# Moving the gate rows and gate columns ahead, and the query split behind a unit, in a hybrid attention and mLSTM layer

## The chip, the cores and the metric

The kernel runs on one core of one Trainium2 chip. The metric is the device time of one execution in microseconds; lower is better. The arithmetic is float32 throughout: matrix products are made as three products of a high part and a low part of each operand (marked float32r), so that every weight and every activation is split before it is used.

## The reference, cut to what matters

One layer of a trunk: a SwiGLU half step, token mixing, a second half step. Token mixing makes one projection of the normalised tokens (640 = 512 latent + 128 context) and runs two mixers on it, a differential attention with 8 heads and a bidirectional mLSTM with 4 heads:

```python
mq, mk, mv, mo, mg, dq, dk, dv, gm, gd = split_cols(h @ p['w_in'][l])
dq = rmsnorm(dq...); dk = rmsnorm(dk...)           # then rope for latent tokens
s = einsum('bqhcd,bkhcd->bhcqk', q, k) * scale      # c = 0, 1
pr = softmax(s); w = pr[:, :, 0] - lam * pr[:, :, 1]
att = einsum('bhqk,bkhv->bqhv', w, v)
gates = (mg + b_gate)                               # 16 columns: log_i, log_f
log_f = log_sigmoid(gates[:, 1])                    # then the mLSTM, chunk by chunk:
b = cumsum(fc); a = b + m
m_t = maximum(a, max(b[t] - b[s] + ic[s]))
```

The change touches the attention heads and the gates of the mLSTM (cumulative sums, running maxima and their exponentials), which the mLSTM needs only after the last attention head.

## The kernel before, in words

The stages follow one another: opening and first half step, input projections by a Strassen-like scheme (class Gates), attention (650 to about 1090 us), mLSTM, branch and output projections, second half step. The change lies in the attention stage.

**Units.** While the heads run, PE is kept full with the remaining input projections, cut into units of 24 matmuls or so: `fill.units(n)` (class Fill, line 1245 on) runs the next n of them. The first 20 are narrow token units (values, keys, queries, values: five each; 128x256, one of four PSUM slots of the pool `psum`). Then come wide units in pairs of halves: the two halves of one token block gather in one 128x512 tile, tag "wide", of which there is one (`wide_ps`); behind the second half ACT copies it out in two pieces. Then units by feature. `fill.ahead` loads and splits weights for later units; a split is a copy on ACT (wH) and a subtraction on DVE (wL). `Fill.one` first does the subtractions that wait (`prefetch(0)`).

**A head** (class Head, line 1650) works in five query blocks. `turn_keys` and `turn_queries` transpose a head's tokens on PE, copy them out on ACT into a tile of tag "asq" (one buffer) and spread them by four DMAs into the tile qk_d. `queries` splits qk_d into qT (one ACT copy, one DVE subtraction), `keys` splits the cached and new keys into kH and kL. `scores(qi)` makes eight matmuls into the one score tile "sc" (three PSUM banks, one buffer) and a minimum on DVE; `soft` the exponentials on ACT; `mix` the combination on DVE; `turn(qi)` the transposes of the mixed weights and their copy on ACT (wT); `values(qi)` the products with the values (ps_o) and their scaling on DVE. `finish` transposes the head's output into aT, again of tag "asq", and stores it.

In block qi the order on PE is scores(qi), turn(qi - 1), n[0] units, values(qi - 1), in blocks 2 and 3 the next head's turn_keys and turn_queries, n[1] units. Behind block 4 stands the boundary to the next head N: N.queries, turn(4), N.keys(0), one unit, values(4), N.keys(1, 2), and two more units (lines 2129 to 2144).

**The gates.** gate_products puts the 16 gate columns into PSUM (ps_g, in the score tile's place). `gate_rows` (line 1426), a generator in six parts, makes of them rows of 640 tokens: sums and logarithms, scans, and at its end stores to DRAM (nm_dram, dc_dram, four stores to qq_dram). `gate_load(j)` (1505) reads half j of qq_dram into QQ, a tile of tag "asq"; `gate_cols` (1508) transposes it on PE (ps_c, five transposes) and copies the columns out on DVE.

**Order.** PE's instructions run as written. What ACT, DVE and SP do is put in order by the framework's planner from its own estimate of durations, except inside `with written():`, where each engine's instructions follow one another as written (`placed`, line 37), and except `tc.issue_after(x)`, which puts instructions behind x on x's engine. So before the loop over the heads the unpinned instructions of units, keys, queries and gate rows are mixed by the planner; the gate rows' first part is held behind the split of head 0's keys and queries (line 2064). Their further parts are called in head 0 by `aside` (ROWS, line 2069), which is called twice in each block, before the n[0] units (part 0) and behind values (part 1). gate_load(0) is called in head 2, block 1, gate_cols in head 2, block 2; the second half in head 4. The pool of the gate rows is closed in head 0, block 2 (`begin_pools`).

Of the kernel before, what the change touches and what calls it, by code (L numbers as in the profile page):

```python
# [8 lines left out]
F32R = mybir.dt.float32r  # L9
# [22 lines left out]
def tile_trunk(ctx: ExitStack, tc: tile.TileContext, a: dict):  # L32
# [17 lines left out]
    def act(*args, **kw):  # L50
        return placed(nc.scalar.activation(*args, **kw))  # L51

    def tt(eng, out, in0, in1, op):
        return placed(eng.tensor_tensor(out=out, in0=in0, in1=in1, op=op))  # L54
# [13 lines left out]
    @contextmanager  # L68
    def written():
        was, as_written[0] = as_written[0], in_row  # L70
        yield
        as_written[0] = was
# [4 lines left out]
    def tr(*args, **kw):  # L77
        tc.keep_in_program_order(nc.tensor.transpose(*args, **kw))  # L78
# [23 lines left out]
    def load(pool, shape, src, **kw):  # L102
        t = pool.tile(shape, F32, **kw)
        dma(t, src)
        return t
# [360 lines left out]
    class HalfStep(Winograd):  # L466
# [102 lines left out]
        def run_first(self, x, gate, final, between, ahead, freed):  # L569
# [107 lines left out]
            for j in range(1, 4):  # L677
                for f in range(2):
                    unit(2, j, f, 1)
                    final(2 * j + f, 1)  # L680

        def run(self, x, gate, final, ahead, aside, add_pair):


# [724 lines left out]
    fill = Fill()  # L1409


    def gate_products():
        raw = load(rawp, [128, KT, 128], a["w_g"], tag="raw", name="wg_raw")
        wgH = wide_p.tile([128, KT, 128], F32R, tag="BH", name="wgH", bufs=2)
        wgL = wide_p.tile([128, KT, 128], F32R, tag="BL", name="wgL", bufs=2)
        act(wgH, raw, AF.Copy)
        tt(vec, wgL, raw, wgH.bitcast(F32), ALU.subtract)
        ps = ps_s.tile([128, 1536], F32, tag="sc", name="ps_g")

        def step(hf, k):  # L1420
            cs = half(hf)
            mm3(ps[:, 512 * hf : 512 * hf + HALF], wgH[:, k, :], wgL[:, k, :], hH[:, k, cs], hL[:, k, cs], k == 0, k == KT - 1)

        return ps, step
# [80 lines left out]
    def gate_load(j):  # L1505
        Q_at[0] = j, load(ap, [128, T], qq_dram[:, j, :], tag="asq", name="QQ")

    def gate_cols():
        j, Q = Q_at[0]
        for i0, n in ((0, 4), (4, 1)):  # L1510
            p = psum.tile([128, 4, 128], F32, tag="mm", name="ps_c")
            for i in range(n):
                tr(p[:, i, :], Q[:, (i0 + i) * 128 : (i0 + i + 1) * 128], ident)
            vec.tensor_copy(
                cols[:, i0 : i0 + n, 2 * j : 2 * j + 2, :].rearrange("p i q (d h) -> p i (q d) h", d=2),
                p[:, :n].rearrange("p i (b c) -> p i b c", c=32)[:, :, :, 0:4],
            )
# [63 lines left out]
    def rotate():  # L1581

        if not rotations:
            return False
        first, second = rotations[0], rotations[1] if len(rotations) > 1 else []
        had, left = len(first), len(second)
        with written():
            if had == 4 and left == 7 or had == 2 and left == 5:
                second.pop(0)()
            else:  # L1590
                first.pop(0)()
                if (had, left) in ((5, 8), (4, 6)):
                    second.pop(0)()
            if not first:
                rotations.pop(0)
        return True
# [53 lines left out]
    class Head:  # L1650
# [28 lines left out]

        def queries(self):  # L1680
            self.qT = ap.tile([128, 2, T], F32R, tag="qT", name="qT")
            self.kH = ap.tile([128, 2, 896], F32R, tag="kH", name="kH")
            self.kL = ap.tile([128, 2, 896], F32R, tag="kL", name="kL")
            self.ao = ap.tile([128, 5, 128], F32, tag="ao", name="ao")
            self.at_q = act(self.qT, self.qd, AF.Copy)
            r = slice(64, 128)
            tt(vec, self.qT[r], self.qd[r], self.qT[r].bitcast(F32), ALU.subtract)

        def keys(self, *parts):
            for n in parts:  # L1690
                c0, c1 = ((512, 768), (0, 512), (768, 896))[n]
                v = (self.ck, self.kd[:, :, 0:NS], self.kd[:, :, NS:T])[n]
                act(self.kH[:, :, c0:c1], v, AF.Copy)
                self.at_vec = tt(vec, self.kL[:, :, c0:c1], v, self.kH[:, :, c0:c1].bitcast(F32), ALU.subtract)
# [92 lines left out]
    def begin_pools():  # L1787
        gates.close()
        late_p.append(late_of.enter_context(tc.tile_pool(name="late", bufs=1, reuse_waits="tile")))
        fill.spare = late_p[0]  # L1790
# [3 lines left out]
    def begin_memory():  # L1794
        assert not rotations and not any(isinstance(g[0], tuple) for g in fill.q)
        fill.spare = None
        late_of.close()
        in_pools["k"] = ctx.enter_context(tc.tile_pool(name="mlk", bufs=1, side="right", reuse_waits="tile"))
        load_keys(0)
        load_queries(0)  # L1800
# [168 lines left out]
    with tc.issue_after(box["normed"]):  # L1969
        ps_g, gate_step = gate_products()  # L1970

    heads = [Head(hd) for hd in range(8)]
# [80 lines left out]
    ap = att.enter_context(tc.tile_pool(name="att", bufs=1, reuse_waits="tile"))  # L2053
    rope_p[0] = ap
    gt = gates.enter_context(tc.tile_pool(name="gates", bufs=1))
    heads[0].load_cache()
    heads[0].turn_keys()
    fill.units(1)
    heads[0].turn_queries()
    fill.units(2)  # L2060
    heads[0].queries()
    heads[0].keys(0, 1, 2)
    fill.units(4)
    with tc.issue_after(heads[0].at_vec.ins), tc.issue_after(heads[0].at_q.ins):
        rows = gate_rows(gt, ps_g)
        next(rows)
    fill.units(2)
    fill.eager = False
    ROWS = {(0, 0): 1, (1, 0): 1, (1, 1): 1, (2, 0): 2}

    def aside(hd, qi, part):
        if hd == 0:
            for _ in range(ROWS.get((qi, part), 0)):
                next(rows, None)
        if part == 0:
            with written():
                split = fill.low()
            if qi < 4 and (UNITS[hd][qi][1] or not split):
                rotate()
        elif qi != 3:  # L2080
            rotate()
        if (qi, part) == (1, 1) and hd in (2, 4):
            gate_load(hd // 2 - 1)
        if (qi, part) == (2, 0) and hd in (2, 4):
            gate_cols()

    two, one = (1, 1), (1, 0)
    UNITS = {hd: (two, one, two, one, one, (1, 1, 1)) for hd in range(7)}
# [3 lines left out]
    for hd in range(8):  # L2092
        H = heads[hd]
        odd = hd % 2
        N = heads[hd + 1] if hd < 7 else None
        for qi in range(5):
            n = UNITS[hd][qi]
            with written():
                H.scores(qi)
                if qi > 0:  # L2100
                    H.turn(qi - 1)
                H.soft(qi)
            aside(hd, qi, 0)
            fill.units(n[0])
            with written():
                H.mix(qi)
            if late is not None and qi == 1:
                with written():
                    late()
                late = None  # L2110
            if qi > 0:
                with written():
                    H.values(qi - 1)
            if qi in (2, 3) and hd < 7:
                with written():
                    (N.turn_keys, N.turn_queries)[qi - 2]()
            if qi == 3 and hd < 7:
                N.load_cache()
            aside(hd, qi, 1)
            if (hd, qi) == (0, 2):  # L2120
                begin_pools()
            elif (hd, qi) == (6, 2):
                begin_memory()
            fill.units(n[1])
            if n[1]:
                rotate()
            with written():
                fill.ahead()
        n = UNITS[hd][-1]
        if hd < 7:  # L2130
            with written():
                N.queries()
                H.turn(4)
                N.keys(0)
            fill.units(n[0])
            with written():
                H.values(4)
                N.keys(1, 2)
            H.finish_norm()
            fill.units(n[1])  # L2140
            with written():
                fill.ahead()
            fill.units(n[2])
            late = H.finish
        else:
            with written():
                H.turn(4)
            fill.eager = True
            fill.units(1)
            H.values(4)  # L2150
            H.finish_norm()
            fill.drain(3)
            with written():
                H.finish()
# [543 lines left out]
```

## Time and profile before

| | us |
|---|---|
| median of three runs | 1822.37 (1822.31 to 1822.61) |
| profiled execution | 1822.42 |
| its span | 1820.6 |
| attention stage, about 650 to 1090: PE busy | 411.4 of 440 |

A row of a timeline has its start in us from the start of the span, the time it took, the engine, the line, the operation, the tile written <- the tiles read, sizes, the number of instructions merged and, in brackets, how long the engine stood idle before it and whose result ended that. In a list of waits the columns are: who waited for whom, the total, how often, the longest. In a table of windows each engine has its busy time and, in parentheses, its instructions; then come the mean granted clock of TensorE (1.00 is full), the share of the DMA engines and the GB/s. PE is TensorE, DVE VectorE, ACT ScalarE, SP the engine that issues most DMAs.

### The profile page before, as it was taken

How to read it: one execution, taken by the hardware profiler on the slowest of the kernel's cores; microseconds unless marked ns; L12 is line 12 of the kernel's file. 1: busy time of each engine (PE TensorE's matmuls, PEld its weight loads, DVE VectorE, ACT ScalarE, POOL GpSimd, SP SyncE). 2: the span in 40 equal slices, each digit the busy share in tenths (PEclk: the TensorE clock that was granted, in tenths of full speed). 3: DMA queues.
4: the chain of work that ended last, by engine and by line, in shares of the span. 5: the costliest groups of instructions: out<-in, count | busy, mean ns of one | idle time of the engine just before them, and what ended most of it. 6: DMA issues, size and time to landing. Idle time of an engine off the chain costs nothing.

```text
span 1820.6 us, 29424 instructions
## 1 busy us (share of the span) xinstructions
PE 1772.2 (97%) x11790; PEld 1706.0 (94%) x11790; DVE 1341.5 (74%) x2136; ACT 894.2 (49%) x1563; POOL 40.8 (2%) x72
## 2 busy tenths in 40 slices
PE   8999999999999998989899999999999999999998
PEld 6999999999999998868788998899999999999998
DVE  6889986677889748667675546876767888997485
ACT  5654553342655445555554536563326545454432
POOL 0000000100000000000000000000000000000010
PEclk9999999999999999999999999999999999999999
DMA  8255566977236554233334336566652445557992
GB/s 331 105 197 185 184 222 237 346 225 258 76 138 202 179 173 105 85 90 107 90 112 129 109 105 234 178 228 212 233 171 80 134 164 193 195 183 272 354 311 82
DMA packets 150075, 328.32 MB, mean 180 GB/s; under 512 B 11633, under 2 KB 107633, under 8 KB 138161
## 3 DMA queue, kind: packets, MB, share of 16 engines
q1 hardware_dynamic: 138562, 280.69, 45.8%
q0 software_dynamic: 10688, 43.13, 7.4%
q10 hardware_dynamic: 688, 2.63, 0.4%
q8 instruction: 92, 1.51, 0.3%
q14 instruction: 45, 0.37, 0.1%
HBM read 243.77 MB, written 72.15 MB: 174 GB/s over the span
## 4 chain that ended last, share of the span: by engine, by line
PE 80%; DMA 7%; DVE 7%; ACT 4%; issue 1%; SPq 1%; ACTq 0%; DVEq 0%
PE ps_f L75 49%; PE ps_p L75 14%; PE ps_t L75 7%; PE sc L75 2%; PE ps_o L75 2%; DVE ww L54 2%; DMA qk_d<-qk_t 1%; PE ps_n L75 1%; DMA P<-nm_dram 1%; DMA raw_a<-in_w_ada_k 1%; DMA raw<-in_w2b 1%; PE ps_wT L78 1%; DVE junk L814 1%; PE ps_u L75 1%; SPq L1668 1%
## 5 line engine op out<-in xcount | busy, mean ns | idle before, releaser
L75 PE MATMUL ps_f<-S,ww 128*128 128x320 f32 x2400 | 387.1, 309 | 2.8 <-DMA S<-g_dram 0.9
L75 PEld LDWEIGHTS ps_f<-S,ww 128*128 128x128 f32 x2400 | 359.8, 188 | 6.9 <-DVE ww L54 4.6
L54 DVE TENSOR_TENSOR ww<-raw,ww 128x2048 fp32r<-128x2048 f32 (+1 forms) x73 | 163.9, 2245 | 66.0 <-ACT ww L51 65.9
L75 PE MATMUL ps_f<-hm,ww 128*128 128x320 f32 x1176 | 185.7, 309 | 0.1
L75 PEld LDWEIGHTS ps_f<-hm,ww 128*128 128x128 f32 x1176 | 175.7, 188 | 0.5 <-DVE ww L54 0.5
L51 ACT ACTIVATE ww<-raw 128x2048 fp32r<-128x2048 f32 (+1 forms) x73 | 136.8, 1875 | 59.2 <-DVE raw L54 34.9
L54 DVE TENSOR_TENSOR raw<-raw 128x1024 f32<-128x1024 f32 x186 | 160.6, 863 | 2.4
L75 PE MATMUL ps_f<-hm,wB 128*128 128x320 f32 x1008 | 161.5, 309 | 0.0
L75 PE MATMUL ps_t<-wH,hH 128*128 128x256 f32 (+1 forms) x440 | 152.8, 347 | 7.4 <-ACT stage L51 2.9
L75 PE MATMUL ps_p<-hH,wH 128*128 128x320 f32 x480 | 150.7, 314 | 1.5 <-DVE num L54 1.5
L75 PEld LDWEIGHTS ps_f<-hm,wB 128*128 128x128 f32 x1008 | 151.3, 188 | 0.0
L75 PE MATMUL ps_t<-wH,hL 128*128 128x256 f32 (+1 forms) x440 | 147.7, 336 | 0.9 <-DVE hL L54 0.9
L75 PE MATMUL ps_p<-hH,wL 128*128 128x320 f32 x480 | 148.3, 309 | 0.0
L75 PE MATMUL ps_p<-hL,wH 128*128 128x320 f32 x480 | 148.3, 309 | 0.0
L75 PE MATMUL ps_t<-wL,hH 128*128 128x256 f32 (+1 forms) x440 | 147.8, 336 | 0.0
L51 ACT ACTIVATE u<-ps_f 128x320 f32<-128x320 f32 x129 | 55.7, 432 | 155.5 <-PE ps_f L75 155.3
L54 DVE TENSOR_TENSOR wL<-raw,wH 128x2048 fp32r<-128x2048 f32 x37 | 84.6, 2287 | 35.5 <-ACT wH L51 34.4
L75 PEld LDWEIGHTS ps_t<-wH,hH 128*128 128x128 f32 x440 | 85.2, 194 | 16.2 <-ACT stage L51 3.5
L51 ACT ACTIVATE wH<-raw 128x2048 fp32r<-128x2048 f32 (+1 forms) x45 | 75.4, 1682 | 50.4 <-PE ps_p L75 36.1
L54 DVE TENSOR_TENSOR wB<-raw,wB 128x1024 fp32r<-128x1024 f32 x64 | 78.0, 1218 | 26.1 <-ACT wB L51 26.1
L814 DVE CUSTOM_DVE_ANT_0 junk<-raw_a,csil 128x1024 bf16<-128x1024 f32 (+1 forms) x76 | 92.5, 1217 | 3.6 <-DMA raw_a<-in_w_ada_c 3.3
L75 PEld LDWEIGHTS ps_t<-wH,hL 128*128 128x128 f32 x440 | 84.8, 193 | 10.1 <-DVE hL L54 1.1
(304 smaller groups left out, 3536.0 us busy)
## 6 DMA issues: line engine op xcount, KB each, us to landing
g_dram<-g SPq DMA_DIRECT2D x44, 640.0 KB, 7.7
raw_a<-in_w_ada_c POOLq DMA_DIRECT2D x38, 512.0 KB, 5.2
g_dram<-g SPq DMA_DIRECT2D x24, 480.0 KB, 8.4
raw<-in_w1b SPq DMA_DIRECT2D x11, 1024.0 KB, 4.9
raw<-in_w3b SPq DMA_DIRECT2D x11, 1024.0 KB, 6.4
raw<-in_w1a SPq DMA_DIRECT2D x10, 1024.0 KB, 4.9
raw<-in_w3a SPq DMA_DIRECT2D x10, 1024.0 KB, 6.1
qk_d<-qk_t SPq DMA_DIRECT2D x64, 160.0 KB, 2.9
```

The costliest lines, as they stand in the source:

```text
L51: return placed(nc.scalar.activation(*args, **kw))
L54: return placed(eng.tensor_tensor(out=out, in0=in0, in1=in1, op=op))
L75: tc.keep_in_program_order(nc.tensor.matmul(*args, **kw))
L78: tc.keep_in_program_order(nc.tensor.transpose(*args, **kw))
L814: placed(vec.tensor_tensor_reduce(out=junk, in0=raw, in1=self.csil[:, v, :], op0=ALU.mult, op1=ALU.add, scale=1.0, scalar=0.0, accum_out=m ...
L1668: nc.sync.dma_start(out=both[64 * r : 64 * r + 64, c, :], in_=t[64 * c : 64 * c + 64])
```

## The change

Four edits. Ahead of the heads, one unit is put before the first turn_keys; the gate rows start right behind it, with no hold, and all six parts run before the first scores, followed by gate_load(0). In head 0, gate_cols runs in part 1 of blocks 0 and 1, with gate_load(1) behind the first; the calls in heads 2 and 4 go. At each boundary N.queries moves from the front to behind the unit, just before values(4), and the unit with its copies joins the written order. The tiles kH and kL are now made by keys(0) and not by queries, which has no instruction of its own. The units before the first scores are nine as before (1, 2, 4, 2 become 1, 1, 1, 2, 2, 2).

```diff
         def queries(self):
             self.qT = ap.tile([128, 2, T], F32R, tag="qT", name="qT")
-            self.kH = ap.tile([128, 2, 896], F32R, tag="kH", name="kH")
-            self.kL = ap.tile([128, 2, 896], F32R, tag="kL", name="kL")
...
         def keys(self, *parts):
+            if 0 in parts:
+                self.kH = ap.tile([128, 2, 896], F32R, tag="kH", name="kH")
+                self.kL = ap.tile([128, 2, 896], F32R, tag="kL", name="kL")
...
     heads[0].load_cache()
+    fill.units(1)
     heads[0].turn_keys()
+    rows = gate_rows(gt, ps_g)
+    next(rows)
     fill.units(1)
     heads[0].turn_queries()
+    next(rows)
+    fill.units(1)
+    next(rows)
+    heads[0].keys(0, 1, 2)
+    heads[0].queries()
     fill.units(2)
-    heads[0].queries()
-    heads[0].keys(0, 1, 2)
-    fill.units(4)
-    with tc.issue_after(heads[0].at_vec.ins), tc.issue_after(heads[0].at_q.ins):
-        rows = gate_rows(gt, ps_g)
-        next(rows)
+    next(rows)
+    fill.units(2)
+    for _ in rows:
+        pass
+    gate_load(0)
     fill.units(2)
     fill.eager = False
-    ROWS = {(0, 0): 1, (1, 0): 1, (1, 1): 1, (2, 0): 2}
 
     def aside(hd, qi, part):
-        if hd == 0:
-            for _ in range(ROWS.get((qi, part), 0)):
-                next(rows, None)
...
-        if (qi, part) == (1, 1) and hd in (2, 4):
-            gate_load(hd // 2 - 1)
-        if (qi, part) == (2, 0) and hd in (2, 4):
+        if (hd, part) == (0, 1) and qi < 2:
             gate_cols()
+            if qi == 0:
+                gate_load(1)
...
         if hd < 7:
             with written():
-                N.queries()
                 H.turn(4)
                 N.keys(0)
-            fill.units(n[0])
+                fill.units(n[0])
             with written():
+                N.queries()
                 H.values(4)
                 N.keys(1, 2)
```

## The prediction

> **What bounds the kernel now.** I read the page first, then the waits of PE, then the timeline of each engine around each wait, and last the granted clock in 4 us windows behind each wait.
>
> ```profile
> span 1820.6 us, 29424 instructions
> ...
> PE 1772.2 (97%) x11790; PEld 1706.0 (94%) x11790; DVE 1341.5 (74%) x2136; ACT 894.2 (49%) x1563; POOL 40.8 (2%) x72
> ```
>
> The profiled execution took 1822.42 us, 1.8 us more than its span, and the median of the runs is 1822.37 us; I count from 1822.4. PE is busy for all but 48.4 us, and the change removes no matmul and no transpose. So it can win only PE's waits and the slow clock behind them. The waits of PE (us in total, times, longest):
>
> ```profile
> PE ps_c L78 <- DMA QQ<-qq_dram: 13.9, 2, 7.3
> PE sc L75 <- ACT p L51: 4.5, 1, 4.5
> ...
> PE ps_t L75 <- ACT stage L51: 2.9, 3, 1.0
> PE ps_o L75 <- ACT wT L51: 2.4, 2, 2.0
> ...
> PE ps_t L75 <- ACT q_tok L51: 2.0, 2, 1.0
> PE ps_t L75 <- ACT g_out L51: 1.6, 1, 1.6
> ```
>
> These six are 27.3 us of the idle time, all in the attention stage, and the diff touches what stands in front of each.
>
> **Gate columns (first row).** The two calls of gate_cols wait for QQ. The chain of waits around the first, and PE's timeline there:
>
> ```profile
> 798.66 6.22 DMA aT_dram<-aT
> ...
> 804.89 2.76 DMA QQ<-qq_dram
> ```
> ```profile
> 807.79 1.30 PE L78 MATMUL ps_c<-ident,QQ 128*128 128x128 f32 x5 [7.33 <-DMA QQ<-qq_dram]
> ```
>
> QQ shares the one buffer "asq" with aT of the head before. Its load can be issued only when the store of aT has landed, 6.22 us, and lands 2.76 us later; PE has one score block to do meanwhile, and the transposes block everything behind them. The change moves both loads to head 0, where no aT exists. So 7.33 us here and 6.6 us at the second call go: 13.9 us.
>
> **Gate rows (second row).** DVE's and PE's timelines in head 0:
>
> ```profile
> 677.34 0.81 DVE L57 SCALAR_TENSOR_TENSOR lf<-fg,e 64x640 f32<-64x640 f32 x1
> ...
> 688.39 0.81 DVE L54 TENSOR_TENSOR e<-u,Ml 64x640 f32<-64x640 f32 x1
> 689.12 1.74 DVE L1716 TENSOR_REDUCE mn<-sc 128x2 f32<-128x1536 f32 x1
> ```
> ```profile
> 692.83 0.80 PE L75 MATMUL sc<-kH,qT 128*128 128x512 f32 x1 [4.54 <-ACT p L51]
> ```
>
> From lf to the end of the subtraction into e, 11.9 us, DVE does gate rows and nothing else. The minimum over the first scores waits behind that, the exponentials behind the minimum, and scores(1) needs the score bank, of which there is one. With the rows issued ahead of the first scores these 4.5 us go, if the rows are through by then; that is taken up below.
>
> **Query split (fourth row).** ACT and PE between head 0 and head 1:
>
> ```profile
> 730.39 1.27 ACT L51 ACTIVATE qT<-qk_d 128x1280 fp32r<-128x1280 f32 x1 [3.95 <-DMA qk_d<-qk_t]
> 731.56 0.26 ACT L51 ACTIVATE wT<-ps_wT 128x128 f32<-128x128 f32 x1
> ```
> ```profile
> 731.88 0.71 PE L75 MATMUL ps_o<-v_tok,wT 128*128 128x128 f32 x2 [1.97 <-ACT wT L51]
> ```
>
> ACT stands 3.95 us at the copy into qT, whose input has not landed; behind it in the fixed order is the copy of the last turned weights, for which values(4) waits. After the change that copy is ahead of the query split, and 1.97 us go. At the next five boundaries the same stall holds up another instruction. ACT, PE and DVE at the one between head 1 and head 2:
>
> ```profile
> 775.13 1.27 ACT L51 ACTIVATE qT<-qk_d 128x1280 fp32r<-128x1280 f32 x1 [3.08 <-DMA qk_d<-qk_t]
> ...
> 778.24 0.37 ACT L51 ACTIVATE k_tok<-ps_t 128x256 f32<-128x256 f32 x1
> 778.50 0.38 ACT L51 ACTIVATE q_tok<-ps_t 128x256 f32<-128x256 f32 x1
> ```
> ```profile
> 777.53 0.38 PE L75 MATMUL ps_o<-v_tok,wT 128*128 128x128 f32 x2
> 778.94 0.50 PE L75 MATMUL ps_t<-wH,hH 128*128 128x512 f32 x1 [1.03 <-ACT q_tok L51]
> ```
> ```profile
> 776.44 1.49 DVE L54 TENSOR_TENSOR qT<-qk_d,qT 64x1280 fp32r<-64x1280 f32 x1 [1.24 <-ACT qT L51]
> ...
> 778.83 1.55 DVE L54 TENSOR_TENSOR kL<-qk_d,kH 128x1024 fp32r<-128x1024 f32 x2
> ```
>
> The wide unit ends at about 777.5, but its two copies start only at 778.24, after queries and keys, and the next wide unit needs the one wide bank. The change puts unit and copies ahead of the queries. The copies take 0.64 us, about 0.75 us with the start, and values(4) covers 0.38 of that: of the 1.0 us some 0.35 stays. Five boundaries (2.9 + 2.0 us in five waits) give 4.9 - 1.75 = 3.2 us.
>
> What is late next there: the queries. Counted from the unit's end: copies to 0.75, qT on ACT to 2.0, its subtraction on DVE to 3.5, the values' scaling (about 0.35) and the key subtractions to 5.4. PE's cover is two units of the kind of the second row:
>
> ```profile
> 701.65 2.87 PE ps_t L75 x24
> ...
> 748.65 2.80 PE ps_t L75 x12
> ```
>
> 0.75 + 2 x 2.8 = 6.35 us. So scores(0) has 0.95 us to spare: no cost, but a thin cover.
>
> **First unit (last row).** PE's timeline at the start of the stage:
>
> ```profile
> 652.08 0.71 PE L78 MATMUL ps_qkT<-ident,k_tok 128*128 128x128 f32 x5
> 654.43 0.38 PE L75 MATMUL ps_t<-wH,hH 128*128 128x256 f32 x1 [1.63 <-ACT g_out L51]
> ```
>
> The transposes of the keys took the first two PSUM slots at once; the unit, third, waited for a slot that a gate product still held. With the unit first it takes the first slot, and the slots wanted 2.9 us later are free: 1.6 us go. The keys' transposes come 2.9 us later on PE but their copy only about 1 us later (it began at 654.8 before), and the queries' likewise; the split of the queries, at 668.6 before, is far from the first scores.
>
> **The clock.** The granted clock behind four of the waits (PE busy, clock):
>
> ```profile
> 692.00:696.00 4.00, 3.17 (x11) 0.50 0.21 43
> 696.00:700.00 4.00, 4.00 (x28) 0.77 0.65 84
> ...
> 732.00:736.00 4.00, 4.00 (x22) 0.57 0.22 60
> ```
> ```profile
> 808.00:812.00 4.00, 4.00 (x16) 0.69 0.00 0
> ```
> ```profile
> 904.00:908.00 4.00, 1.88 (x7) 0.50 0.29 82
> 908.00:912.00 4.00, 4.00 (x20) 0.81 0.00 0
> ```
>
> Busy time times the missing clock: 1.6 + 0.9 behind the scores; 1.7 behind values(4); 1.2 and 0.9 + 0.8 behind the two gate columns. Sum 7.1 us, which go with their waits. The 1.6 us wait and the 1.0 us waits cost no clock.
>
> [...]
>
> **What it adds: a wait at the new place.** The rows cannot start before their pool's memory is free of the gate products; its first write, MP, waited for that. The rows of the chain are these (DVE, ACT, SP):
>
> ```profile
> 658.14 0.06 DVE L1472 MEMSET MP<- 64x5 f32 x1 [1.16 <-DMA gm_dram<-g_out]
> ...
> 675.13 2.29 DVE L54 TENSOR_TENSOR wL<-raw,wH 128x2048 fp32r<-128x2048 f32 x1 [3.79 <-ACT wH L51]
> ```
> ```profile
> 669.73 0.51 ACT L51 ACTIVATE fg<-ps_g,b_g 64x320 f32<-64x320 f32 x1
> ```
> ```profile
> 690.05 0.45 SPq L1494 DMA_DIRECT2D qq_dram<-e x1
> ```
>
> Before, fg to lf took 677.34 - 669.73 = 7.6 us, with a weight split (wL, 2.29) in it. Starting at 658.1, lf comes at 663 (that split away) to 665.7. To the end of e's subtraction it is 11.9 us of DVE, and in between DVE now also has the query subtraction (1.49), and at most the keys' (about 2.2) and that weight split: 1.5 to 6.0 us. So e's subtraction ends at 676.4 to 683.6. From there the exponential to the issue of its store took 0.85 us (689.20 to 690.05); the store takes about as long as the load of QQ, 2.8 us at most by that row, then the load 2.8: QQ lies in SBUF at 682.8 to 690.0. On SP the nine transfers of the rows and the two of QQ now come ahead of the first scores or soon after. A load of QQ that waits there holds back the weight loads queued behind it; those are for the wide units, which begin after twenty narrow ones, nine before the first scores and eleven in head 0, so a hold of a few us costs nothing; without that cover it would cost its full length.
>
> PE reaches gate_cols(0) after nine units (25.8), ten transposes (1.3), scores (1.4 by the eight matmuls at full clock, an estimate from 0.28 to 0.40 each, overlapping) and one more unit (2.9): 652.1 + 31.4 = 683.5. The wait is 0 to 6.5 us; I take 3.1, about the middle, and for the clock behind it 1.7, what the 2.0 us wait cost: 4.8 us. Queued behind it are the next unit and scores(1). The second QQ is loaded when the first is read, and PE has two units and scores until it is needed: no wait. The ten gate transposes cost the same in head 0; in heads 2 and 4 they had been slow.
>
> **Sum.** 13.9 + 4.5 + 2.0 + 3.2 + 1.6 + 7.1 = 32.3 us gone, 4.8 added: 27.5 us, or 1794.9 us. Nothing else bounds behind it: a stretch that is mostly head 3, without gate columns, has PE busy for 51.0 of 52 us and DVE for 36.5.
>
> ```profile
> 842.00:894.00 52.00, 51.01 (x285) 43.81 (x283) 36.50 (x53) 31.67 (x65) 0.00 (x0) 1.00 0.36 108
> ```
>
> **Rivals.**
>
> A: the rows don't come early. Their instructions are not pinned, so the planner may leave fg where ACT had it, behind the split of the queries at 669.7. Then e's subtraction ends at 689.2 as before, QQ lies there at 695.6, and PE stands 12.1 us at gate_cols(0), which takes in the old wait at scores(1), with 2.5 us of clock. The saving is 32.3 - 14.6 = 17.7: 1804.7 us. For it: the planner has its own durations. Against it: nothing holds fg back in the new code but the pool's memory. Chance 0.20.
>
> B: slower. A weight split (ACT 1.9, DVE 2.3, as in wL) falls into the fixed row between the unit and the queries at each of seven boundaries, since the unit's own call may split what it finds waiting. The queries come 4.2 us later, scores(0) 3.2 us late with 1.7 us of clock: 4.9 x 7 = 34 us, against 27.5 + the lost 3.2 of the boundaries: 1822.4 - 24.3 + 34 = 1832. It turns the sign when the queries are later than the cover by about 1.8 us with clock (3.5 x 7 = 24.3). Against it: at these boundaries the trace has the splits behind the key copies. Chance 0.06.
>
> C: given back. The memory stage behind the heads or its loads are late by themselves, and half is lost: 1808 us. Against it: those loads are released by PE's own progress. Chance 0.06.
>
> D: no change: the planner orders ACT and DVE as before nearly everywhere, so that the diff does not do what it says, and A and the half of C meet. Chance 0.04.
>
> **The numbers.** My forecast, 1788 to 1803, has 0.64. Its low end is no new wait at all and nothing left at the boundaries: 1822.4 - 32.3 - 1.75 = 1788.3; its high end is the wait of 6.5 us and no gain at the first unit or the boundaries: 32.3 - 8.2 - 4.8 = 19.3, or 1803.1. With A the range is 1788 to 1807. About 0.2% (3.6 us) is what a measurement can tell: faster 0.90 (forecast, A and C), same 0.04 (D), slower 0.06 (B).
>
> **What would show it.** Right: no ps_c rows in heads 2 and 4, the wait for QQ in head 0 under 7 us, no wait of sc on ACT p, wT's copy ahead of qT's, clock 1.00 from 730 to the end of the heads. Wrong: fg later than 665, a wait of sc for qT or kL at the head boundaries, or saved waits that come back behind 1060 us.

## The result, and the profile after

The changed kernel took 1805.45 us (median of four runs, 1802.33 to 1808.09), the kernel before 1822.49 us (four runs, 1822.31 to 1823.25): a ratio of 0.9905 [0.9886, 0.9924], 17.0 us faster. I had forecast 27.5 us, so it is faster, mostly by the means I named, and ten microseconds of the gain are missing. The profiled execution took 1802.33 us, the shortest of the four.

The head of the page of after, then the waits of PE, with the columns as before (who waited for whom: total, times, longest):

```profile
span 1800.5 us, 29431 instructions
...
PE 1768.4 (98%) x11790; PEld 1701.7 (95%) x11790; DVE 1339.7 (74%) x2136; ACT 893.6 (50%) x1563; POOL 40.8 (2%) x72
```
```profile
PE ps_aT L78 <- DVE ao L54: 4.7, 3, 2.3
PE ps_qkT L78 <- ACT v_tok L51: 2.3, 1, 2.3
PE ps_t L75 <- ACT stage L51: 1.9, 4, 0.6
PE ps_t L75 <- ACT q_tok L51: 1.4, 3, 0.5
...
PE ps_qkT L78 <- ACT qk_t L51: 0.6, 1, 0.6
PE ps_o L75 <- ACT wT L51: 0.5, 1, 0.5
```

PE's idle time, span less busy time, fell from 48.4 to 32.1 us, and its busy time by 3.8: together the 20.1 us between the two profiled executions. The rows of the two loads of QQ (13.9), of the second scores (4.5) and of the gate product (1.6) are gone, and 1.9 of the 2.0 us at values(4). Of the 4.9 us behind the wide unit's two copies 3.3 are left, where I expected 1.75. And there are waits in two places that the prediction does not have: 4.7 us of the transposes of a head's normalised output, ps_aT, and 2.3 + 0.6 us of the transposes of the first queries, ps_qkT.

The two executions differ ahead of the stage too, where the diff changes nothing: ACT's last table load before it (ACT_TABLE_LOAD, line 84) starts at 647.46 us in before and at 649.60 in after, and most of this shift is there within the first 50 us. I call the time from this load to the first product into ps_n, behind the heads, the stage. It takes 452.9 us in before and 431.9 in after, 21.0 less. Every start time of after below is late by these 2.1 us.

**The gate rows.** DVE, then PE, at the start of the attention stage of after:

```profile
665.75 0.82 DVE L57 SCALAR_TENSOR_TENSOR lf<-fg,e 64x640 f32<-64x640 f32 x1 [3.68 <-ACT e L51]
...
679.79 0.81 DVE L54 TENSOR_TENSOR e<-u,Ml 64x640 f32<-64x640 f32 x1
```
```profile
688.88 0.71 PE L78 MATMUL ps_c<-ident,QQ 128*128 128x128 f32 x5
```

lf comes at 665.75 (predicted 663 to 665.7, without the late start) and e's subtraction ends at 680.6 (predicted 676.4 to 683.6). PE takes QQ at 688.88 without a bracket: no wait. The new wait was put at this place, and it is somewhere else. ACT, then PE, a little earlier:

```profile
660.36 0.52 ACT L51 ACTIVATE fg<-ps_g,b_g 64x320 f32<-64x320 f32 x1 [3.32 <-DMA gm_dram<-g_out]
...
662.52 0.38 ACT L51 ACTIVATE v_tok<-ps_t 128x256 f32<-128x256 f32 x1
```
```profile
662.96 0.66 PE L78 MATMUL ps_qkT<-ident,q_tok 128*128 128x128 f32 x4 [2.29 <-ACT v_tok L51]
```

fg stands 3.32 us on ACT until the memory of its pool is free. Behind it on ACT, in order, wait the first unit's copy out of PSUM and the copy of the turned keys. The four PSUM slots fill, and the turn of the queries finds none until that copy is through: PE stands 2.29 us, with the queries and everything behind them.

**The boundary.** One of the two worst places is between head 2 and head 3, about 817 to 838 us. ACT, DVE and PE of after:

```profile
816.85 0.38 ACT L51 ACTIVATE v_tok<-ps_t 128x256 f32<-128x256 f32 x1 [2.00 <-PE ps_t L75]
...
820.63 1.92 ACT L51 ACTIVATE wH<-raw 128x2048 fp32r<-128x2048 f32 x1 [0.71 <-PE ps_t L75]
822.46 0.72 ACT L51 ACTIVATE asq<-ao 128x640 f32<-128x640 f32 x1
```
```profile
818.71 1.49 DVE L54 TENSOR_TENSOR qT<-qk_d,qT 64x1280 fp32r<-64x1280 f32 x1 [2.67 <-ACT qT L51]
820.23 0.35 DVE L61 TENSOR_SCALAR ao<-ps_o,rc 128x128 f32<-128x128 f32 x1
...
822.58 2.29 DVE L54 TENSOR_TENSOR wL<-raw,wH 128x2048 fp32r<-128x2048 f32 x1 [0.54 <-ACT wH L51]
824.79 0.81 DVE L1763 TENSOR_REDUCE ass<-asq 128x5 f32<-128x640 f32 x1
...
833.41 2.28 DVE L54 TENSOR_TENSOR wL<-raw,wH 128x2048 fp32r<-128x2048 f32 x1
...
837.06 0.82 DVE L54 TENSOR_TENSOR ao<-ao,ry 128x640 f32<-128x640 f32 x1
```
```profile
837.94 0.76 PE L78 MATMUL ps_aT<-ident,ao 128*128 128x128 f32 x5 [2.29 <-DVE ao L54]
```

And the same boundary of the kernel before, ACT, DVE and PE:

```profile
832.55 0.37 ACT L51 ACTIVATE v_tok<-ps_t 128x256 f32<-128x256 f32 x1
...
833.32 0.74 ACT L51 ACTIVATE asq<-ao 128x640 f32<-128x640 f32 x1
...
836.32 1.92 ACT L51 ACTIVATE wH<-raw 128x2048 fp32r<-128x2048 f32 x1 [0.44 <-PE ps_t L75]
```
```profile
832.89 0.34 DVE L61 TENSOR_SCALAR ao<-ps_o,rc 128x128 f32<-128x128 f32 x1
...
844.07 0.82 DVE L54 TENSOR_TENSOR ao<-ao,ry 128x640 f32<-128x640 f32 x1
```
```profile
850.57 0.71 PE L78 MATMUL ps_aT<-ident,ao 128*128 128x128 f32 x5
```

Count both from the copy of the wide unit (816.85 and 832.55). The weight split wH starts 3.8 us after it in both. The scaling of the last values, ao, ended 0.7 us after it before, and 3.7 us after it now, because DVE does the query subtraction first and waits 2.67 us for its input. So the square of the output, asq, which came well ahead of the split, now comes behind it on ACT; the sum ass comes behind wL on DVE, and the small steps of the norm, which end in ao, behind a second wL. The normalised ao is ready 12.3 us after the copy before and 21.0 us now; PE comes for it at 18.0 and at 18.8. A slack of 5.7 us has become a wait of 2.29 us, at two of the seven boundaries. The square comes behind wH at all five boundaries from head 1 to head 6, but only at these two is the second wL ahead of the norm's last step as well; at the other three PE waits 0.16 us or nothing.

### The profile page after: what moved, and what is told of

Same layout as the page of the kernel before. It is cut to its first block, busy times and chain, and to the rows that moved or that the text cites. A ratio compares the mean times of both kernels' runs of the same rounds, so it can differ in the third digit from the quotient of the medians.

```text
span 1800.5 us, 29431 instructions
## 1 busy us (share of the span) xinstructions
PE 1768.4 (98%) x11790; PEld 1701.7 (95%) x11790; DVE 1339.7 (74%) x2136; ACT 893.6 (50%) x1563; POOL 40.8 (2%) x72
## 4 chain that ended last, share of the span: by engine, by line
PE 84%; DVE 8%; DMA 4%; ACT 3%; issue 1%; SPq 0%; ACTq 0%; DVEq 0%
PE ps_f L75 49%; PE ps_p L75 14%; PE ps_t L75 9%; PE ps_o L75 2%; PE sc L75 2%; PE ps_n L75 2%; DVE ww L54 2%; DMA raw_a<-in_w_ada_k 1%; PE ps_wT L78 1%; DMA P<-nm_dram 1%; PE ps_u L75 1%; DVE wL L54 1%; DMA raw<-in_w2b 1%; DVE junk L814 1%; DVE mn L1717 1%
```

## The experiments

My theory after the result: the gate part does what was predicted, and the missing time is lost at the boundary edit, which delays the output norm. Rivals: the stall at the first queries, or saved time given back behind the heads.

**The changed kernel again**, for a second profile and more runs.

> The changed kernel once more. Its four runs lay between 1802.3 and 1808.1 us, the kernel before between 1822.3 and 1823.3. Theory one: the spread comes from the clock; three waits of 2.3 to 2.9 us (queries' transposes, two output transposes) sometimes cost clock behind them and sometimes not, so a slower run has the same waits and a lower mean clock: 1802 to 1808 again, about 1.2 to 1.7 us for each wait that is hit. Theory two: the spread comes from waits of other lengths (loads), so the waits themselves differ by several us between profiles at the same clock.

1804.29 us (1801.90 to 1806.23), ratio 0.9902 [0.989, 0.9915]. Its profiled execution took 1806.23 us, 3.9 more than the first one. The waits of the stage agree within 0.1 us. What differs is the clock behind them. Windows (busy times, clock) and the timeline of PE in this profile:

```profile
836.00:840.00 4.00, 1.70 (x8) 1.28 (x7) 2.84 (x8) 0.36 (x2) 0.00 (x0) 0.86 0.51 161
840.00:844.00 4.00, 4.00 (x24) 3.77 (x23) 1.35 (x2) 0.95 (x2) 0.00 (x0) 0.71 0.50 183
```
```profile
838.89 1.33 PE L78 MATMUL ps_aT<-ident,ao 128*128 128x128 f32 x5 [2.30 <-DVE ao L54]
```

The same wait of 2.3 us at the same place; the transposes behind it took 1.33 us against 0.76, and 1.4 us of clock are missing (1.70 x 0.14 + 4.00 x 0.29). In the first profile both windows have 1.00. Over the whole stage 4.6 us of clock are missing here and none in the first profile, and the stage takes 436.3 us and 431.9. So one kernel runs 1802 to 1808 us with the same waits.

**The boundary edit alone**, on the kernel before; at head 0 the keys go ahead of the queries, since they now make the tiles.

```diff
             with written():
-                N.queries()
                 H.turn(4)
                 N.keys(0)
-            fill.units(n[0])
+                fill.units(n[0])
             with written():
+                N.queries()
                 H.values(4)
```

> The kernel before with the boundary edit alone (query split behind the unit, the unit in the written order). Theory one: it removes 2.0 us and 1.7 us of clock behind head 0 and about 2 us of the five 1.0 us waits, but it delays the scaling of the last values and with it the output norm, so the output transposes of two heads wait 2.3 us each: net gain 0 to 2 us, 1820.5 to 1822.5. The prediction's account (thin cover that holds, nothing else late): 6.9 us gained, 1815.5. In both, the waits for QQ stay at about 14 us.

1827.46 us, ratio 1.003 [1.0019, 1.0041]: alone, it makes the kernel slower by 5.3 us. The waits of PE:

```profile
PE ps_c L78 <- DMA QQ<-qq_dram: 14.4, 2, 7.6
...
PE ps_aT L78 <- DVE ao L54: 4.7, 3, 2.3
```

The ps_aT row is there, with the size it has in after. Against before: 4.7 + 0.5 (QQ) added, 1.9 + 1.6 gone, 1.7 us worse. The span is 4.4 us longer. Of that, 2.0 us lie ahead of the stage (the table load starts at 649.46), where no edited line runs. The stage takes 455.8 us against 452.9 and has less clock missing, 6.4 us against 7.3, summed over 4 us windows as in the prediction: with the missing clock taken off it is 3.8 us longer. The expectation, 1820.5 to 1822.5, was too low.

**The gates alone**: the changed kernel with the old boundary, the diff above turned round.

> The changed kernel with the boundary as it was before (queries first, the unit outside the written order). Theory one: the gate parts carry the gain: 13.9 + 4.5 + 1.6 us of waits and 5.4 us of clock go, 2.9 us come at the queries' transposes; no 2.3 us waits of the output transposes: 1799 to 1802, no slower than the changed kernel. Rival: the output transposes wait because PE now reaches them earlier, without the waits for QQ, and the boundary edit is worth 5 us: then the 2.3 us waits stay and it takes 1807 or more.

1801.03 us (1800.12 to 1804.13), ratio 0.9888 [0.9875, 0.9901]; in the same set of runs as the changed kernel's 1804.29. The waits of PE:

```profile
PE ps_t L75 <- ACT stage L51: 2.9, 3, 1.0
PE ps_o L75 <- ACT wT L51: 2.5, 2, 2.0
PE ps_t L75 <- ACT q_tok L51: 2.0, 2, 1.0
PE ps_qkT L78 <- ACT v_tok L51: 2.1, 1, 2.1
```

No ps_aT; the waits at the boundary are those of before. The gain without the edit is 21.1 us, and with it 17.9 in this set. These four rows and 0.6 us of qk_t sum to 10.1 us, the six rows of after to 11.4; 1.3 us is thus the edit's price in waits. The price in time is 3.3 us in this set (4.4 against the first set's 1805.45), and the two intervals overlap, so the sign rests on the boundary edit alone. The stage agrees with it: it takes 430.0 us here with 1.5 us of clock missing, and 431.9 and 436.3 in the two profiles of the changed kernel, with 0 and 4.6 missing. With that taken off, the edit costs 3.2 to 3.4 us. The rows of waits show less than half of that; the rest lies in time that the profile counts as busy, and its cause stays open. The clock behind the two ps_aT waits comes on top, 2.9 us in one profile and none in the other.

**The rows held back**, so that fg does not stand ahead of the first copies on ACT. The hold is behind the first unit's copy and the keys' copy:

```diff
     rows = gate_rows(gt, ps_g)
-    next(rows)
+    with tc.issue_after(at_v[0].ins), tc.issue_after(heads[0].at_turned.ins):
+        next(rows)
```

> The changed kernel with the first part of the gate rows held on ACT behind the first unit's copy and behind the copies of the turned keys. Theory one: the 2.9 us at the queries' transposes come from fg standing on ACT for its pool's memory with the first unit's copy behind it; with the hold they go: 2.9 us less, up to 4.5 with clock, while gate_cols(0) still waits for nothing. Rival: the gates' chain or the queries get later, and the wait comes back at gate_cols(0) or at the first scores: no change in time.

1811.71 us, ratio 0.9945 [0.9933, 0.9957]: 7.4 us slower than the changed kernel beside it. The waits of PE:

```profile
PE ps_c L78 <- DMA QQ<-qq_dram: 3.5, 1, 3.5
PE ps_t L75 <- ACT qk_t L51: 3.4, 1, 3.4
```

The 2.3 + 0.6 us are gone, and 3.5 + 3.4 have come. In the timeline ACT now stands 4.54 us at the copy of the turned queries into qk_t, since the keys' transfer out of that buffer lands only at 668.8; the copy frees PSUM slots, and PE finds none for the next unit (the 3.4 us of the list). The rows' first steps are no later for the hold (lf at 664.30, in an execution whose stage starts 0.9 us earlier), but e's subtraction ends at 683.6, 3.0 us later than in the changed kernel, and PE now waits for QQ. Why the keys' transfer lands no earlier, though it was issued some 6 us earlier than in the changed kernel, stays open.

**The norm put into the written order**, to cure ps_aT:

```diff
                 N.keys(1, 2)
-            H.finish_norm()
+            with written():
+                H.finish_norm()
```

with the sum ass placed in that order too.

> The changed kernel with the output norm of each head (finish_norm) in the written order, behind the key copies and ahead of the next weight split and the next head's first minimum. Theory one: the two 2.3 us waits of the output transposes come because the norm's small steps fell behind a weight split and pinned work; pinned they go: 4.7 us less and up to 3 us of clock, about 1799 us. Rival: the pinned chain stalls DVE and ACT for the logarithm and exponential and the first scores of the next head pay: the waits move to scores, 1804 or more.

1814.30 us, ratio 0.9958 [0.9945, 0.997]: slower than the changed kernel. The first row of the waits of PE:

```profile
PE ps_t L75 <- DVE wL L54: 10.1, 4, 3.3
```

There is no ps_aT row any more: the norm was the cause. But ACT now does asq (820.64) before wH (824.03, in after 820.63), and the units wait 10.1 us for the split. The cure only changed who is late.

**The values ahead of the queries**: unit and copies first, as in the change, but then the last values.

```diff
             with written():
-                N.queries()
                 H.values(4)
+                N.queries()
                 N.keys(1, 2)
```

> The changed kernel with values(4) written ahead of the query split at each boundary, so that DVE scales the last values before it subtracts for the queries. Theory one: what makes the norm late is that scaling, which stands behind the query subtraction (1.5 us); with it ahead the square on ACT comes before the weight split again and the 2.3 us waits go: about 1799 to 1801 us. Rival: the place of the weight split alone decides (the planner puts it ahead in any case): the waits stay and the time is that of the changed kernel, 1804 to 1805.

1795.50 us (1794.03 to 1798.22), ratio 0.9859 [0.9844, 0.9874]: the best of all, 26.3 us under the kernel before in its set of runs, and better than the 1799 to 1801 expected. The waits of PE, and DVE at the boundary:

```profile
PE ps_qkT L78 <- ACT v_tok L51: 2.5, 1, 2.5
PE ps_t L75 <- ACT stage L51: 1.6, 3, 0.6
```
```profile
816.52 0.35 DVE L61 TENSOR_SCALAR ao<-ps_o,rc 128x128 f32<-128x128 f32 x1 [1.04 <-PE ps_o L75]
818.14 1.49 DVE L54 TENSOR_TENSOR qT<-qk_d,qT 64x1280 fp32r<-64x1280 f32 x1 [1.28 <-ACT qT L51]
821.14 0.81 DVE L1763 TENSOR_REDUCE ass<-asq 128x5 f32<-128x640 f32 x1
822.01 2.29 DVE L54 TENSOR_TENSOR wL<-raw,wH 128x2048 fp32r<-128x2048 f32 x1
...
828.07 0.81 DVE L54 TENSOR_TENSOR ao<-ao,ry 128x640 f32<-128x640 f32 x1
```

The scaling fits into the time in which DVE waited for the queries anyway. The sum comes ahead of the split, the normalised output at 828.9 and not 837.9, and no ps_aT row is left. No wait of sc for the queries appears either.

**Gate columns alone**, on the kernel before, placed where the buffer is free (block 0 of heads 2 and 4) and not in head 0:

```diff
-        if (qi, part) == (1, 1) and hd in (2, 4):
+        if (qi, part) == (0, 0) and hd in (2, 4):
             gate_load(hd // 2 - 1)
-        if (qi, part) == (2, 0) and hd in (2, 4):
+        if (qi, part) == (0, 1) and hd in (2, 4):
             gate_cols()
```

> The kernel before with the two loads of QQ put into block 0 of heads 2 and 4, ahead of the aT that shares their buffer, and the gate columns behind the first unit of that block; the gate rows and the boundaries stay as they were. Theory one: the 13.9 us of waits go but for 0 to 2 us, and 3 us of clock with them: 1805.5 to 1807.5. So the place of the load alone carries most of the gain, and the early gate rows add 4.5 + 1.6 + 2.5 - 2.9 = some 5 us. Rival: aT, which now waits for QQ to be read, or the transposes in a busier block give it back: 1812 or more.

1804.44 us, ratio 0.9904 [0.9891, 0.9918]: 17.4 us, for 13.9 of waits and 3.0 of clock in the prediction. No row of ps_c waits for QQ. So the place of the load behind the shared buffer is shown as the cause, and these two changed conditions bring as much as the whole change.

**PE kept busy in that wait**: 48, then 24 matmuls of 128x128 into a tile that nobody reads, ahead of the gate columns of the kernel before, to price the clock by itself.

```diff
         j, Q = Q_at[0]
+        idle = psum.tile([128, 4, 128], F32, tag="mm", name="ps_idle2")
+        for _ in range(24):
+            mm(idle[:, 0, :], ident, ident, start=True, stop=True)
```

> The kernel before with 48 extra matmuls of 128x128 in front of each of the two sets of gate transposes (they write a PSUM tile that nobody reads; nothing is left out). Each set is about 5.3 us of PE work inside a wait of about 7 us. Theory one: the wait for QQ stays as it is in sum, but PE's clock stays full behind it, so the 1.3 and 1.7 us of missing clock go: about 3 us less, 1819. Rival: the clock behind the waits is not worth that (the matmuls behind them wait for other things anyhow): no change, 1822; or the extra work lengthens the path: over 1823.

1828.61 us, ratio 1.004 [1.0028, 1.0053]. It was mis-sized: a set took 10.88 us and the wait is 7.3, so it tells little of the clock. With 24:

> As the run with 48 extra matmuls, but with 24 in front of each set of gate transposes. The 48 took 10.88 us, longer than the wait; 24 take 5.4 us and fit into the 7 us. Theory one: the wait and the extra work together end when QQ lands, as before; the clock behind stays full: 1.3 and 1.7 us of missing clock go, about 3 us less than the kernel before. Rival: the missing clock behind these waits costs nothing, since the matmuls there wait for other things: no change.

1820.64 us (1817.66 to 1824.16), ratio 0.9994 [0.9984, 1.0004]: no verdict from the time, since the executions scatter by more than the 3 us in question. The profile says more; PE at the first set (a matmul here leaves two records, so 24 are x48), and the window behind it:

```profile
802.42 5.52 PE L75 MATMUL ps_idle<-ident 128*128 128x128 f32 x48
809.82 0.73 PE L78 MATMUL ps_c<-ident,QQ 128*128 128x128 f32 x5 [1.87 <-DMA QQ<-qq_dram]
```
```profile
808.00:812.00 4.00, 2.19 (x12) 1.93 (x13) 1.14 (x3) 0.00 (x0) 0.00 (x0) 1.00 0.27 79
```

With the wait cut to 1.87 us the clock stays at 1.00, where it had been 0.69. The stage is 3.3 us shorter than in before, near the 3 us expected, but that does not price this clock: 5.9 us less of it are missing in all, the rest at values(4) and behind the scores, and other waits grew.

**Values first, and the rows held** behind the first unit's copy alone:

```diff
-    next(rows)
+    with tc.issue_after(at_v[0].ins):
+        next(rows)
```

> The kernel with values(4) ahead of the query split (1795.5 us) and the first part of the gate rows held on ACT behind the first unit's copy alone, not behind the keys' copies. Theory one: the 2.8 us in front of the queries' transposes and the clock behind them (1.2) go, and nothing comes at gate_cols(0), since the keys' copies keep their place: 1791.5 to 1793. Rival: as in the run with both holds, the wait comes back at a later unit or at gate_cols(0): 1795 or more.

1800.23 us, ratio 0.9877 [0.986, 0.9894], not better than 0.9859 without the hold (in another set of runs, and the intervals overlap). The waits of PE:

```profile
PE ps_c L78 <- DMA QQ<-qq_dram: 4.5, 1, 4.5
...
PE ps_qkT L78 <- ACT qk_t L51: 1.3, 1, 1.3
```

The 2.5 + 0.3 us at the first queries have become 1.3 there and 4.5 at the first gate columns. In both attempts, holding the rows later has only moved the stall; I take it as the price of having them early.

## Why the prediction was right or wrong

The measured 1805.45 us lies above the forecast of 1788 to 1803. It lies in the wider 1788 to 1807 only because rival A widened that, and it is close to A's 1804.7, but A did not happen: that agreement is luck. None of the signs listed for being wrong appeared either; the loss came at a reader that the list does not have.

**Gate columns: right.** 13.9 + 3.0 = 16.9 us predicted, 17.4 measured alone.

**Gate rows: right in size, wrong in place.** The second scores' wait went, and the rows lie where the bounds put them. The step that failed is "The wait is 0 to 6.5 us; I take 3.1" at gate_cols(0), 4.8 us with its clock. That wait is zero. In its place PE stands 2.9 us at the first queries, by ACT's queue and the PSUM slots. I had named the cause, fg waiting for its pool's memory, but listed what stands behind it on DVE and SP, not on ACT, where fg itself stands. The stall and the missing wait are linked: the load of QQ is issued at 684.62 and the two loads take 3.0 to 3.8 us to land, so QQ is there 0.5 to 1.3 us before PE comes at 688.88. Without the 2.9 us PE would have waited for it some 1.6 to 2.4 us, an estimate from these rows, and in the last experiment, where the rows are held and the stall is shorter, it does wait, 4.5 us. So the sum came out nearly right with the stall in another place. For the gate part the terms come to 27.5 - 6.9 = 20.6 us, and 21.1 were measured. Part of that is luck: in the gates' profile the wait at values(4) is still there, but the 1.7 us of clock behind it, which are not among these terms, went as well. Over the columns alone the rest of the gate part brings some 3 us (0.9888 against 0.9904; the intervals overlap).

**Query split and unit: wrong in sign.** Predicted were 2.0 + 1.7 + 3.2 = 6.9 us of gain. In waits the edit takes away 1.9 + 1.6 and brings 4.7, and the time is 3.3 to 4.4 us longer with it than without; this difference, some 10 to 11 us, accounts for what is missing from the forecast. The sentence that failed is "So scores(0) has 0.95 us to spare: no cost, but a thin cover". The cover did hold: no wait of sc is left in after. But I asked only whether the queries come late for their reader. What the queries were moved ahead of, values(4), comes late too, and behind that the norm and its reader ps_aT, 18 us later. I listed the values' scaling in that chain (about 0.35 us) and didn't follow its own consumer. Putting values first gives 5.3 us over the old boundary (0.9859 against 0.9888), near the 6.9 predicted: the idea of the edit was sound, its order was not.

**Clock: right in one execution, too large in the other.** 7.1 us were to go. Summed over the windows of the stage, 7.3 us were missing in before, none in the first profile of after and 4.6 in the second, 2.9 of these behind the two ps_aT waits and 1.7 behind the wait at the first queries. So 7.3 or 2.7 us went. Both profiles of after miss another 1.4 us, nearly all in the first 40 us of the span, where before misses none and the diff changes nothing.

**Rivals.** A did not happen: fg ran at 660.36, and no wait for QQ is left. B foresaw the boundary as the place of a loss, by a split ahead of the queries in the fixed row; the splits are not there, but they do come ahead of the norm. C did not happen: from the first instruction into ps_n, behind the heads, to the end of the span it is 720.3 us before and 719.0 after. D did not happen.

## What to carry to other kernels

When a step is moved past another in a fixed order, follow the consumers of both: here the values' scaling, which was passed, came 3.0 us later with 2.67 us of the queries' input wait ahead of it, and for what it feeds PE came 18.8 us behind the unit's copy and had to wait 2.29 us. An instruction that may wait for memory can hold up the PSUM copies behind it on its engine, and PE with them: here fg stood 3.32 us on ACT, and PE 2.29 us for a copy behind it. List these copies before moving such an instruction. Whether to hold it back has to be timed: here both holds made the kernel no faster. Two moves in one diff are best timed one at a time: here one gives 21 us and the other takes 4 back, and a swap of two lines gets those 4 and 5 more.

## What the runs showed of the hardware

In these runs the length of a short wait of PE, 2.0 to 2.5 us, did not decide whether clock was missing behind it. The wait of 1.97 us at values(4) was followed by a window at 0.57 in before; in the gates-alone kernel it is the same wait at another time, PE and the window behind it, at 1.00:

```profile
729.12 0.49 PE L75 MATMUL ps_o<-v_tok,wT 128*128 128x128 f32 x2 [1.99 <-ACT wT L51]
```
```profile
732.00:736.00 4.00, 4.00 (x34) 3.91 (x33) 3.10 (x8) 1.43 (x5) 0.00 (x0) 1.00 0.21 70
```

In the gate-columns-alone kernel that wait, 2.13 us, had 0.57 behind it again, and with the 24 extra matmuls, at 2.47 us, it had 1.00; the 2.3 us waits at ps_aT had 1.00 in the first profile of the changed kernel and 0.71 and 0.77 in the second. The prediction took 1.7 us for such a wait as a price; in these profiles it was a stake of 0 to 1.7. What decides it was not shown.
